# Attention over 64 heads: eleven pairs transposed by transfers inside SBUF, thirteen groups of scores on VectorE

## The chip, the cores and the metric

The kernel runs on one core of a Trainium2 chip. The metric is the device time of one execution in microseconds (us); a kernel's time is the median of several runs. A profiled execution gives the trace that is quoted here. The engines are called PE (matmuls; PEld is its weight load), ACT (exponentials), DVE (elementwise work), POOL (casts) and SP (issues transfers).

## What is computed

Plain attention for batch 8, 8 heads, 512 positions, dimension 64, in float32. So there are 64 independent heads.

```python
scores = np.einsum('bhqd,bhkd->bhqk', q, k) * scale
scores = scores - scores.max(axis=-1, keepdims=True)
attn = np.exp(scores)
attn = attn / attn.sum(axis=-1, keepdims=True)
return np.einsum('bhqk,bhkd->bhqd', attn, v)
```

The kernel leaves out the subtraction of the maximum, which changes nothing in exact arithmetic, and divides by the sum at the end: the values carry a column of ones, so that the sum comes out of the same matmul.

## The kernel before

**Pairs, groups, units.** The 64 heads are worked on as 32 pairs g. For each pair, q, k and v come from memory as one transfer per tensor (256 KB, `load`, L536 to L542, issued by SP), are cast to fp16 by POOL (`cast`, L544; v into `vp` at L548, q and k side by side into one tile `qkp` at L565), and q and k are transposed, so that the dimension lies along the partitions (`tqk`).

**Two ways to transpose.** Pairs 1 to 28 go through PE: `transposes` (L582 to L592) issues two sets of four 128x128 transposes into a PSUM bank, and `copy` (L601) brings the result to `tqk` with one DVE copy. Pairs 29 to 31 (`FLIPPED = 29`) go through `flip` (L594 to L599): one transposing transfer on SP's queue from `qkp` to `tqk`, both in SBUF. Pair 0 has a written-out start (`first_pair`).

**Scores.** A group m is two 128x512 blocks of scores (keys by queries), one of each head of the pair, four groups to a pair (m // 4 is the pair). PE writes it into one of three PSUM buffers `st` (`scores`, L618, matmuls at L642). ACT then takes the exponential of the whole group, `pt<-st`, at L647. That is the rule; the groups listed in `Plan.ON_DVE` have their exponential made on DVE instead, from a polynomial and the bits of the number: PE first adds a constant (the lift, L628), then `raise_` (L665) and three passes (`pass_`, L687) follow on DVE, with the result in `pd`. Each of them reads or writes 128x1024 elements. For a group in `Plan.SHARED` the middle pass runs on POOL (`middle`, L700 and L703). For a group in `SHARED` or `FREED` the score buffer comes free after the first pass, otherwise after the second. For a pair with such a group POOL also scales part of k (L564).

**Values.** For each head, four units of four matmuls multiply 128x128 pieces of the exponentials by v (`values`, L740), seven units to a PSUM bank; two banks `x0`, `x1` are shared by these and by the transposes. DVE takes the reciprocal of the sums (L708) and multiplies (L716) into a ring of 56 units in SBUF, from which SP stores finished heads (L731). ACT may run far ahead of the values: there are 30 `pt` tiles.

**The order of the work.** Nothing is scheduled at run time. The class `Plan` steps through a model of the engines in time, with its own constants for what each operation costs, and writes down a list of steps; the loop at the end of the kernel issues them in that order, and each engine works through its own queue in that order, waiting where data is not there. So the constants at the head of `Plan` decide which instruction stands ahead of which on each engine. The ones that the change touches:

- `due` (in `__init__`) sorts the casts: k and q of a pair are due `lead` before its scores (2300 ns, or `LEAD` = 8000 for a flipped pair), v later.
- `emit` writes down a cast; behind the cast of a flipped pair's q it writes the flip, and behind each cast the load that takes over the raw buffer (7 pairs later, `RAW`). From the time `CALM` on, a cast is made to wait for the DVE instruction before it (`cast_behind`, L577).
- `fits` holds a cast of q or k back until pair g - 5 is transposed (five `qkp` tiles).
- `step_sp` models SP's queue in order: a flip waits for both casts, and what stands behind it waits too.
- `step_pe` chooses between scores, transposes and values; `KEEN` is the group before which no values are begun; `HURRY`, `SOON`, `BACKLOG` say how long PE holds back for scores.
- `step_dve` chooses among copies, reciprocals, normalisations, raises and passes; `LATE_COPY`, `LATE_NORM`, `LATE_MULT` say how long these may be put off for a pass, and `ROOM` when a reciprocal is issued ahead of its multiplication.

```python
# the tiles between the steps (inside the kernel function)
lpool = ctx.enter_context(tc.tile_pool(name="load", bufs=7))
qpool = ctx.enter_context(tc.tile_pool(name="qk16", bufs=5))
tpool = ctx.enter_context(tc.tile_pool(name="tqk", bufs=6))
ppool = ctx.enter_context(tc.tile_pool(name="pt", bufs=30))
```

Of the kernel before, what the change touches and what calls it, by code (L numbers as in the profile page):

```python
# [17 lines left out]
class Stores:  # L18

    def __init__(self, pairs, units):  # L20
        self.pairs, self.units = pairs, units
        self.started = []
        self.waiting = []
# [24 lines left out]
class Plan:  # L48
# [7 lines left out]
    COPY_1 = (400, 190)  # L56
    NORM_COLUMN, PASS_DONE = 67, 80
    RECIP, RECIP_DONE, CHAINED = 80, 230, 117
    APART, ROOM = 1, -400
    PASS, PASSES = 1131, 3  # L60
    OFFSET = 216
    FIRST_EXP = 5130
    STEP = 5
    CALM, KEEN = 14000, 6
    FIRST_UNIT, FIRST_VALUES = 4, 6000
    ON_DVE = (9, 18, 28, 39, 49, 57, 68, 79, 89, 94, 103, 111)
    SHARED = (39, 49, 89, 103)
    FREED = (94, 111)

    LATE_NORM, LATE_MULT, LATE_COPY, HURRY, SOON, BACKLOG = 1300, 1600, 2200, 800, 40, 1500  # L70
    SLACK, AHEAD = 200, 2

    CAST, CAST_DONE, TO_POOL = 560, 130, 150
    SCALED, MORE = 595, 75
    MIDDLE, MIDDLE_DONE = (1120, 2300), 250
    FIRST_LAND, LOAD, STORE, LATENCY, ISSUE, FLIP_ISSUE = 5200, 700, 350, 2300, 540, 1490
    RAW, QK16, NV = 7, 5, 12
    FLIPPED, LEAD, FLIP = 29, 8000, 3500
    RING = 56

    def __init__(self, groups, pairs, first):
        self.groups, self.pairs = groups, pairs
        self.pe, self.act, self.dve = 6500, self.FIRST_EXP, 6500
        self.pool, self.port, self.dma = 4900, 4900, self.FIRST_LAND
        self.m, self.tiled = first, True
        self.buffers = [1e9] * 3
        self.buffer = {}
        self.exps = {}
        for m in range(first):
            self.act += self.EXP + self.EXP_FIXED  # L90
            self.exps[m] = self.buffers[m] = self.act + self.EXP_DONE
        self.tq = {0: 5800}
        self.transposed = {0: 5800}
        self.next_t = 1
        self.part_t = 0
        self.banks = [5100, 5800]
        self.todo = [(g, h) for g in range(pairs) for h in range(2)]
        self.last = self.todo.pop()
        self.last_part = 0
        self.head = None  # L100
        self.stores = Stores(pairs, self.RING)
        self.units = self.FIRST_UNIT
        self.member = {b: m for m, grp in enumerate(groups) for b in grp}
        self.ready = []
        self.passes = []
        self.steps = []
        self.busy_dve = 0
        self.done_heads = 0

        late = {grp[0][0] for m, grp in enumerate(groups) if m in self.ON_DVE}  # L110
        due = []
        for g in range(pairs):
            scores = 5000 + 3380 * g
            if g:
                lead = self.LEAD if g >= self.FLIPPED else 2300
                due += [(scores - lead, g, "k"), (scores - lead + 10, g, "q")]
            values = 4000 if g else self.FIRST_VALUES
            due.append((scores + values + (6000 if g in late else 0), g, "v"))
        self.due = sorted(due)
        self.extra = {}  # L120
        for m in self.ON_DVE:
            g = groups[m][0][0]
            self.extra[g] = self.extra.get(g, self.SCALED - self.MORE) + self.MORE
        self.uncast = list(self.due)
        self.casts = []
        self.landed, self.cast_done = {}, {}
        self.first_loads = [(g, n) for _, g, n in self.due if g < self.RAW]
        self.first_loads += [(self.RAW, "k"), (self.RAW, "q")]
        for x in self.first_loads:
            self.dma += self.LOAD  # L130
            self.landed[x] = self.dma
        self.loads = []
        self.sp = 1650 + 470 * len(self.first_loads)
# [4 lines left out]
    def released(self, m):  # L138
        return 0 if m in self.SHARED or m in self.FREED else 1

# [3 lines left out]
    def emit(self, t, after):  # L144
        _, g, n = self.uncast.pop(0)
        shared = (g, n) == (1, "q")
        self.note(t, "cast", g, n, t > self.CALM)
        if not shared:
            self.casts.append((g, n, t if after is None else after + self.TO_POOL))
        if n == "q" and g >= self.FLIPPED:  # L150
            self.note(t, "flip", g)
            self.loads.append(("flip", g))
        if g + self.RAW < self.pairs:
            self.note(t, "load", g + self.RAW, n)
            self.loads.append(("load", g + self.RAW, n))
# [25 lines left out]
    def step_sp(self, t):  # L181
        if not self.loads or self.sp > t:
            return
        what = self.loads[0]
        if what[0] == "flip":
            g = what[1]
            if any(self.cast_done.get((g, n), 1e9) > t for n in "kq"):
                return
            self.dma = max(self.dma, t + 1600) + 1000
            self.tq[g] = self.transposed[g] = max(self.dma, t + self.FLIP)  # L190
            self.loads.pop(0)
            self.sp = t + self.FLIP_ISSUE
            return
        elif what[0] == "load":
            _, g, n = what
            if g >= self.RAW and self.cast_done.get((g - self.RAW, n), 1e9) > t:
                return
            self.dma = max(self.dma, t + self.LATENCY - self.LOAD) + self.LOAD
            self.landed[(g, n)] = self.dma
        else:  # L200
            if what[1] > t:
                return
            self.dma = max(self.dma, t + self.LATENCY - self.STORE) + self.STORE
        self.loads.pop(0)
        self.sp = t + self.ISSUE
# [11 lines left out]
    def for_dve(self, m):  # L217
        return m in self.ON_DVE

# [29 lines left out]
    def transposes(self, t):  # L249
        if self.part_t == 0:  # L250
            self.bank_t = self.bank(t)
            self.banks[self.bank_t] = 1e9
        self.note(t, "transposes", self.next_t, self.part_t, self.bank_t)
        self.full(t, self.TRANSPOSE)
        self.part_t += 1
        if self.part_t == 2:
            self.transposed[self.next_t] = self.pe + self.TO_DVE
            self.ready.append((self.pe + self.TO_DVE, "copy", (self.next_t, self.bank_t)))
            self.next_t += 1
            self.part_t = 0  # L260

    def wants(self, g, h, part):
# [66 lines left out]
    def step_pe(self, t):  # L329
        if self.m == len(self.groups):  # L330
            self.values(t)
            return
        g = self.groups[self.m][0][0]
        backlog = self.act - t
        one, two = self.free() <= t, self.free(1) <= t
        if one and (two or backlog < self.HURRY or self.tiled):
            return self.scores(t)
        if not one and backlog < self.BACKLOG and self.free() < t + self.SOON:
            return
        if self.part_t:  # L340
            return self.transposes(t)
        if (
            self.next_t < min(self.pairs, self.FLIPPED)
            and self.next_t <= g + self.AHEAD
            and all(self.cast_done.get((self.next_t, n), 1e9) <= t for n in "kq")
            and self.bank(t) is not None
        ):
            return self.transposes(t)
        if not self.values(t) and one:
            self.scores(t)  # L350

    def step_dve(self, t):
# [56 lines left out]
        elif any(x[2] <= t for x in self.passes):  # L409
# [5 lines left out]
            if all(x[0] > end - late[x[1]] for x in self.ready):  # L415
# [11 lines left out]
                del self.passes[after]  # L427
                if s == 0 and m in self.SHARED:
                    self.passes.remove((m, 1, 1e9))
# [24 lines left out]
def kernel(  # L454
# [28 lines left out]
    raises = {}  # L483
    for m in Plan.ON_DVE:
        (g, c, _), (g2, c2, _) = groups[m]
# [3 lines left out]
    cpool = ctx.enter_context(tc.tile_pool(name="const", bufs=1))  # L489
    lpool = ctx.enter_context(tc.tile_pool(name="load", bufs=7))  # L490
    qpool = ctx.enter_context(tc.tile_pool(name="qk16", bufs=5))
    tpool = ctx.enter_context(tc.tile_pool(name="tqk", bufs=6))
    ppool = ctx.enter_context(tc.tile_pool(name="pt", bufs=30))
    dpool = ctx.enter_context(tc.tile_pool(name="pd", bufs=4))
    wpool = ctx.enter_context(tc.tile_pool(name="work", bufs=2))
# [15 lines left out]
    tqk = {}  # L511
# [61 lines left out]
    def dve(ins):  # L573
        latest[:] = [ins]
        return ins
# [99 lines left out]
    def pass_(m, s):  # L675
# [7 lines left out]
        last = s == 2  # L683
        shared = m in Plan.SHARED
        one = low if m not in Plan.FREED else f
        dve(
# [196 lines left out]
    with tc.manual_schedule():  # L883
# [10 lines left out]
        for n in range(NV):  # L894
            nc.vector.memset(vps[n][:, :, :, D : D + 1], 1.0)
        first_pair()
        do = {
            "transposes": transposes,
            "flip": flip,
            "scores": scores,  # L900
# [45 lines left out]
```

## Time and profile before

| | us |
|---|---|
| median of three runs | 117.22 (116.72 to 117.48) |
| the profiled execution | 117.66 |
| its span, first to last instruction | 115.9 |
| ACT busy | 108.4 |
| PE busy | 105.5 |
| DVE busy | 100.2 |
| POOL busy | 75.8 |

The profiled execution is 0.44 us above the median, and 1.8 us of it lie outside the span. In the lines that follow, a group of instructions shows its line in the kernel, engine and operation, what it writes and reads, its count, then busy time and the mean duration of one in ns, then the idle time of its engine ahead of it and what ended that. A line of a timeline begins with the start and the duration in us; consecutive instructions of a kind are merged. A line of windows shows for each engine the busy time in that stretch and the number of instructions, in the order PE, PEld, DVE, ACT, POOL, then the granted clock of PE, the share of the DMA engines that was busy (it can be over 1 where packets overlap) and GB/s. The granted clock was 1.00 throughout.

### The profile page before, as it was taken

The numbers are of one execution on the slowest core, as the hardware profiler recorded it, in microseconds if no ns is written. First come the engines' busy times: TensorE is split into PE (matmuls) and PEld (weight loads), VectorE is DVE, ScalarE is ACT, GpSimd is POOL, SyncE is SP. The second block draws the span as 40 slices with busy tenths as digits, with TensorE's granted clock in tenths as the row PEclk, the third lists the DMA queues.
The fourth block names the chain that finished last, engine by engine and source line by source line (L and its number), as shares of the span: only waits on it lengthen the run. The fifth ranks groups of instructions, "written<-read, shape, count | busy, mean of one in ns | idle before, by whom it ended". The sixth has DMA issues, their size and how long they took to land.

```text
span 115.9 us, 4036 instructions
## 1 busy us (share of the span) xinstructions
PE 105.5 (91%) x1558; PEld 65.8 (57%) x1558; DVE 100.2 (86%) x181; ACT 108.4 (94%) x120; POOL 75.8 (65%) x122
## 2 busy tenths in 40 slices
PE   7978989989998999999899998989999989799980
PEld 2454655556573668665575664756566556467660
DVE  4752599999999978999999999999999997997481
ACT  2589999999999999999999999999999999999980
POOL 2339965895985985999676949948792849821000
PEclk9999999999999999999999999999999999999999
DMA  3899999999999999999999999999927598026443
GB/s 91 293 305 373 384 379 382 384 377 381 363 384 374 375 378 374 369 371 359 351 380 375 385 377 311 375 367 377 382 100 206 182 119 224 2 96 228 145 159 112
DMA packets 38581, 34.61 MB, mean 299 GB/s; under 512 B 5409, under 2 KB 38561, under 8 KB 38561
## 3 DMA queue, kind: packets, MB, share of 16 engines
q1 hardware_dynamic: 37984, 34.02, 88.3%
q10 hardware_dynamic: 576, 0.33, 0.9%
q8 instruction: 12, 0.20, 0.7%
q14 instruction: 9, 0.07, 0.2%
HBM read 25.17 MB, written 8.39 MB: 290 GB/s over the span
## 4 chain that ended last, share of the span: by engine, by line
ACT 48%; PE 35%; issue 6%; DMA 5%; POOL 2%; SPq 2%; DVE 1%; ACTq 0%
ACT pt L647 48%; PE o L740 15%; PE st L642 14%; PE tp L590 5%; DMA k<-in_k_dram 5%; SPq L785 1%; POOL qkp L565 1%; PE st L628 1%; SPq L542 1%; DVE obl L771 1%; POOL vp L548 0%; POOL k L564 0%; DVE rc_last L770 0%; PE o_last L756 0%; ACTq L647 0%
## 5 line engine op out<-in xcount | busy, mean ns | idle before, releaser
L647 ACT ACTIVATE pt<-st 128x1024 f16<-128x1024 f32 (+1 forms) x114 | 103.9, 1153 | 0.3 <-PE st L642 0.3
L642 PE MATMUL st<-tqk 64*128 64x512 f16 (+1 forms) x250 | 46.1, 380 | 4.4 <-ACT pt L647 3.2
L740 PEld LDWEIGHTS <-pt 128*128 128x128 f16 x912 | 36.0, 98 | 15.9 <-issue 14.7
L740 PE MATMUL o<-vp,pt 128*128 128x65 f16 x912 | 43.9, 194 | 0.3 <-POOL vp L548 0.2
L548 POOL CAST vp<-v 128x512 f16<-128x512 f32 x32 | 19.4, 619 | 8.1 <-DVE pd L687 4.7
L716 DVE TENSOR_TENSOR ring<-o,rc 128x448 f32<-128x448 f32 (+2 forms) x37 | 22.6, 611 | 1.2
L642 PEld LDWEIGHTS <-tqk 64*128 64x128 f16 x250 | 13.4, 93 | 15.4 <-issue 7.0
L565 POOL CAST qkp<-k 128x512 f16<-128x512 f32 x31 | 19.0, 614 | 4.4 <-PE st L642 1.6
L565 POOL CAST qkp<-q 128x512 f16<-128x512 f32 x30 | 18.5, 616 | 5.0 <-DVE y L687 1.7
L610 DVE COPY tqk<-tp 128x1024 f16<-128x1024 f16 x27 | 18.3, 679 | 3.1 <-PE tp L590 3.1
L590 PE MATMUL tp<-ident,qkp 128*128 128x128 f16 x224 | 17.9, 220 | 0.6 <-DVE tqk L610 0.4
L590 PEld LDWEIGHTS <-qkp 128*128 128x128 f16 x224 | 12.8, 97 | 7.7 <-issue 3.6
L665 DVE TENSOR_SCALAR z<-st 128x1024 f32<-128x1024 f32 x12 | 14.6, 1218 | 2.0 <-PE st L642 2.0
L687 DVE SCALAR_TENSOR_TENSOR pd<-y,z 128x1024 uint32<-128x1024 f32 x12 | 15.1, 1258 | 0.0
L740 PE MATMUL o<-vp,pd 128*128 128x65 f16 x96 | 14.8, 195 | 0.0
L687 DVE SCALAR_TENSOR_TENSOR y<-st,z 128x1024 f32<-128x1024 uint16 x12 | 14.5, 1212 | 0.1
L740 PEld LDWEIGHTS <-pd 128*128 128x128 f16 x96 | 9.4, 98 | 1.3 <-issue 1.3
L708 DVE RECIPROCAL rc<-o 128x7 f32<-128x7 f32 (+2 forms) x37 | 7.2, 196 | 2.9 <-PE o L740 2.9
L703 POOL TENSOR_TENSOR y<-t,y 128x1024 f32<-128x1024 f32 x4 | 9.5, 2363 | 0.3
L564 POOL TENSOR_SCALAR k<-k 128x128 f32<-128x128 f32 x12 | 6.4, 530 | 4.2 <-DVE pd L687 2.5
L687 DVE SCALAR_TENSOR_TENSOR y<-st,y 128x1024 f32<-128x1024 uint16 x6 | 7.3, 1214 | 0.0
L628 PE MATMUL st<-const-bfloat16-1.0,lift 64*128 64x512 bf16 x24 | 4.6, 380 | 1.0 <-ACT pt L647 1.0
(57 smaller groups left out, 35.5 us busy)
## 6 DMA issues: line engine op xcount, KB each, us to landing
v<-in_v_dram SPq DMA_DIRECT2D x32, 256.0 KB, 5.4
k<-in_k_dram SPq DMA_DIRECT2D x31, 256.0 KB, 5.4
q<-in_q_dram SPq DMA_DIRECT2D x31, 256.0 KB, 5.4
out_dram<-ring SPq DMA_DIRECT2D x25, 256.0 KB, 4.9
out_dram<-ring SPq DMA_DIRECT2D x13, 128.0 KB, 4.6
k<-in_k_dram ACTq DMA_DIRECT2D x2, 64.0 KB, 2.4
q<-in_q_dram SPq DMA_DIRECT2D x2, 64.0 KB, 2.2
q<-in_q_dram SPq DMA_DIRECT2D x1, 128.0 KB, 3.2
```

The source lines that it names most:

```text
L548: return nc.gpsimd.tensor_copy(out=vps[g % NV][:, :, :, 0:D], in_=raw[g]["v"][:, :, :, :])
L565: ins = nc.gpsimd.tensor_copy(out=dst, in_=src[:, :, :, :])
L590: nc.tensor.transpose(tps[g][:, n, i, :], qkp[g][:, n, i, :], ident)
L610: nc.vector.tensor_copy(out=tqk[g][:, :, :], in_=tps.pop(g).rearrange("p n i c -> p n (i c)"))
L642: nc.tensor.matmul(st[:, x, cols], kc, qc[:, cols], start=not on_dve, stop=True)
L647: nc.scalar.activation(out=pt[:, :, cols], in_=st[:, :, cols], func=EXP, scale=scale)
L665: nc.vector.tensor_scalar(out=r["z"][:, :, :], in0=r["st"][:, :, :], scalar1=128.0, scalar2=2.0**17, op0=AluOp.mult, op1=AluOp.max,)
L687: nc.vector.scalar_tensor_tensor(out=r["bits"][:, :, :] if last else y, in0=(low, one, y)[s], scalar=(QUARTIC if shared else CUBIC)[s], in ...
L703: nc.gpsimd.tensor_tensor(out=y[:, :, :], in0=t[:, :, :], in1=y[:, :, :], op=AluOp.mult)
L708: dve(nc.vector.reciprocal(out=rcs[u][:, 0:n], in_=o[:, x : x + n, D : D + 1]))
L716: nc.vector.tensor_tensor(out=ring[:, u % NU : u % NU + n, :], in0=o[:, x : x + n, 0:D], in1=rc[:, 0:n].broadcast_to([P, n, D]), op=AluOp. ...
L740: nc.tensor.matmul(os[u // 7][:, u % 7, :], blocks[(g, c, h)][:, y * P : (y + 1) * P], vps[g % NV][:, h, c, :], start=(c == 0), stop=(c == ...
```

## The change

Eleven pairs, and not the last three alone, are transposed by transfers: 14, 17, 20, 22, 24 and 26 to 31. There are thirteen groups on DVE for twelve, at other places; two of them, and not four, share their middle pass with POOL, and four, not two, are in `FREED`. The planner's account of a transposing transfer is 1400 ns of the queue's time and 500 ns behind it, for 1000. Other constants of the planner change as listed, and `tqk` has ten buffers for six. The instructions themselves stay as they are.

```diff
-    APART, ROOM = 1, -400
+    APART, ROOM = 1, 600
...
-    CALM, KEEN = 14000, 6
+    CALM, KEEN = 9000, 7
     FIRST_UNIT, FIRST_VALUES = 4, 6000
-    ON_DVE = (9, 18, 28, 39, 49, 57, 68, 79, 89, 94, 103, 111)
-    SHARED = (39, 49, 89, 103)
-    FREED = (94, 111)
-
-    LATE_NORM, LATE_MULT, LATE_COPY, HURRY, SOON, BACKLOG = 1300, 1600, 2200, 800, 40, 1500
-    SLACK, AHEAD = 200, 2
+    ON_DVE = (8, 18, 28, 38, 45, 55, 65, 70, 80, 91, 97, 105, 112)
+    SHARED = (65, 97)
+    FREED = (55, 91, 105, 112)
+
+    LATE_NORM, LATE_MULT, LATE_COPY, HURRY, SOON, BACKLOG = 1600, 1600, 1400, 800, 0, 800
+    SLACK, AHEAD = 300, 2
...
-    FLIPPED, LEAD, FLIP = 29, 8000, 3500
+    FLIPPED = (14, 17, 20, 22, 24, 26, 27, 28, 29, 30, 31)
+    LEAD, FLIP = 8000, 3500
...
-                lead = self.LEAD if g >= self.FLIPPED else 2300
+                lead = self.LEAD if g in self.FLIPPED else 2300
...
-        if n == "q" and g >= self.FLIPPED:
+        if n == "q" and g in self.FLIPPED:
             self.note(t, "flip", g)
             self.loads.append(("flip", g))
...
-            self.dma = max(self.dma, t + 1600) + 1000
-            self.tq[g] = self.transposed[g] = max(self.dma, t + self.FLIP)
+            self.dma = max(self.dma, t + 1600) + 1400
+            self.tq[g] = self.transposed[g] = max(self.dma + 500, t + self.FLIP)
...
             self.next_t += 1
+            while self.next_t in self.FLIPPED:
+                self.next_t += 1
...
-            self.next_t < min(self.pairs, self.FLIPPED)
+            self.next_t < self.pairs
...
-    tpool = ctx.enter_context(tc.tile_pool(name="tqk", bufs=6))
+    tpool = ctx.enter_context(tc.tile_pool(name="tqk", bufs=10))
```

## The prediction

> **What bounds the kernel now.** I read the page first (busy time, then the chain that ended last), then the timeline of ScalarE, then busy times by stage, then the groups of what the change touches, and last the transfers around the three transposing ones that exist already.
>
> The page:
>
> ```profile
> PE 105.5 (91%) x1558; PEld 65.8 (57%) x1558; DVE 100.2 (86%) x181; ACT 108.4 (94%) x120; POOL 75.8 (65%) x122
> ...
> DMA  3899999999999999999999999999927598026443
> ...
> ACT 48%; PE 35%; issue 6%; DMA 5%; POOL 2%; SPq 2%; DVE 1%; ACTq 0%
> ```
>
> See that ACT and PE share the chain, that DVE is at 86% only because it idles at both ends, and that the DMA engines are full until slice 29 (85 us).
>
> ScalarE's timeline, whole and in a stretch without gaps:
>
> ```profile
> 8.35 5.62 ACT L647 ACTIVATE pt<-st 128x1024 f16<-128x1024 f32 x6
> 14.26 98.25 ACT L647 ACTIVATE pt<-st 128x1024 f16<-128x1024 f32 x108 [0.28 <-PE st L642]
> ...
> 19.70 5.66 ACT L647 ACTIVATE pt<-st 128x1024 f16<-128x1024 f32 x6
> ```
>
> Exponentials overlap: one of them lasts about 1.15 us, and six take 5.66 us, so a new one starts every (5.66 - 1.15) / 5 = 0.90 us. At that step 106 whole ones from 14.26 us on take 95.8 us, the two half ones about 1.2 us, together 97.0 of 98.25 us: ACT never stands idle long, and late starts cost it 1.2 us in all. ACT bounds the kernel. What can be won is the exponentials taken from it and those 1.2 us.
>
> Busy times by stage:
>
> ```profile
> 15.00:50.00 35.00, 33.09 (x506) 21.11 (x506) 33.34 (x51) 35.00 (x40) 26.92 (x44) 1.00 1.08 376
> 50.00:85.00 35.00, 33.53 (x506) 21.00 (x503) 34.33 (x52) 35.00 (x40) 27.70 (x42) 1.00 1.06 364
> 85.00:105.00 20.00, 18.30 (x292) 11.66 (x293) 19.16 (x30) 20.00 (x23) 12.42 (x17) 1.00 0.53 124
> 105.00:116.00 11.00, 7.60 (x151) 5.34 (x147) 5.59 (x15) 7.51 (x10) 0.00 (x0) 1.00 0.50 165
> ```
>
> Columns: PE, PEld, DVE, ACT, POOL busy, granted clock, DMA share, GB/s. DVE (third) has 1.7 us of idle time from 15 to 50 us and 1.5 us from 50 to 105. PE has 1.9 and 3.2.
>
> **The change part by part.** The groups it touches:
>
> ```profile
> L610 DVE COPY tqk<-tp 128x1024 f16<-128x1024 f16 x27 | 18.3, 679 | 3.1 <-PE tp L590 3.1
> L590 PE MATMUL tp<-ident,qkp 128*128 128x128 f16 x224 | 17.9, 220 | 0.6 <-DVE tqk L610 0.4
> L687 DVE SCALAR_TENSOR_TENSOR pd<-y,z 128x1024 uint32<-128x1024 f32 x12 | 15.1, 1258 | 0.0
> L703 POOL TENSOR_TENSOR y<-t,y 128x1024 f32<-128x1024 f32 x4 | 9.5, 2363 | 0.3
> ```
>
> *One more group of scores on VectorE (13 for 12).* ACT loses one exponential: -0.90 us on the path. DVE gains a group. PE gains two lift matmuls (the chain has two as 0.22 us), beside the rest.
>
> *DVE's sum.* Its instructions overlap a little: by its timeline a pass starts the next 1.13 us later and a copy 0.60 us later. A group takes four instructions (raise and three passes), a shared one three, the middle pass being POOL's. Before: 8 x 4 + 4 x 3 = 44. After, with two shared: 11 x 4 + 2 x 3 = 50. So 6 x 1.13 = +6.8 us, and eight copies fewer, 8 x 0.60 = -4.8 us: +2.0 us against 3.2 us of idle time from 15 to 105 us. It is uneven. Groups 38 and 45 stand where shared 39 and 49 stood, so the first half gains two passes, +2.3 us, against 1.7 us of idle time and the 0.9 us that starting at group 8 and not 9 opens. The second half gains 4 x 1.13 = 4.5 and loses 4.8. DVE is then full from 13 us to 105 us; I cost this at nothing because what waits for it (normalised outputs, last passes) has PE's backlog of values between it and ACT. If that cover is gone, each us of DVE too many is a us of the end (below).
>
> *Transposes off PE.* Eight pairs more (14, 17, 20, 22, 24, 26, 27, 28) lose eight transposes each; the chain shows such a set as 0.55 us, so PE loses 4.4 us and gains 0.22, all of it after 45 us. This is off ACT's path except where ACT starts late for want of scores. Of the 1.2 us of late starts, some 0.9 lie after 45 us, in about eight places of 0.1 each, most at a group that DVE holds. Bounds: nothing, if all come from the buffer that DVE holds, and -0.9, if all come from PE's load. I take -0.4, between the ends, since the chain does run through PE at those places (57.5 to 69.9, 82.3 to 89.1, 104.3 to 109.4 us). A thirteenth place of the kind: +0.1.
>
> *POOL.* Two middles fewer, 2 x (1.05 + 2.36) = -6.8 us, one scaling of k more, +0.53: off the path at 65%.
>
> *Planner constants, casts and queues.* Values begin one group later, casts wait for DVE from 9 us on, the limits for late copies and norms move. A flipped pair's casts are due 8.0 us before its scores, not 2.3, so they go ahead of those of an unflipped pair before it, and the loads issued behind those casts move with them. On POOL nothing is added. The one stretch where such order shows in ACT is 13 to 14.3 us, 0.4 us late: -0.4 to +0.4, taken at zero, as no row tells the sign. Ten tqk buffers for six cost nothing and take away a wait of transfers for scores long done.
>
> *The eight transfers.* What the three that exist did, by SP's timeline:
>
> ```profile
> 86.28 1.33 SPq L596 DMA_TRANSPOSE tqk<-qkp  x1
> 87.71 4.24 SPq L731 DMA_DIRECT2D out_dram<-ring  x5
> 92.24 4.24 SPq L596 DMA_TRANSPOSE tqk<-qkp  x2
> ```
>
> By the transfers' line, their landing after issue:
>
> ```profile
> DMA to landing us min/median/max: 2.8/2.9/4.5
> ```
>
> By windows of 1 us (last columns: DMA share, GB/s):
>
> ```profile
> 93.00:94.00 1.00, 0.89 (x17) 0.57 (x14) 1.00 (x2) 1.00 (x3) 0.35 (x1) 1.00 1.85 202
> 94.00:95.00 1.00, 0.63 (x6) 0.36 (x6) 1.00 (x3) 1.00 (x3) 0.40 (x1) 1.00 0.98 38
> ```
>
> Each holds SP 1.3 us, once 2.6 (a load 0.4 to 0.7), so SP gains 8 x 1.3 = 10 us, while a full DMA queue of some 5 us (loads land 5.4 us after issue) covers each. The first one, alone, moved its packets in 1.1 us; the second, behind stores, had the DMA engines nearly stuck for a us (38 GB/s) and took about 3. So eight cost 8.8 to 24 us of DMA time. The DMA engines have room: after 85 us they move 3.5 MB of stores, 9.3 us at 376 GB/s, and three transfers, 5.2 us, which leaves 28 - 14.5 = 13.5 us before 113 us. And loads lie early: by issue and landing, pair 14's keys land at 34 us for scores at 51, pair 24's at 62 for 84, pair 31's at 82 for 108. I take 1.1 to 1.7 us each (the mean of the three is 5.2 / 3), 8.8 to 13.6 us, hidden.
>
> The Trainium skill's page "Advanced Engine Details and Errata", section "X-Bar Transpose (TRN2)", says that a transposing transfer is as fast as a plain one. The trace disagrees: 1.1 us against 0.70 us for the same 262 KB at 376 GB/s; by the page eight would take 5.6 us, and nothing else here would change.
>
> Sum: -0.90 - 0.4 + 0.1 = -1.2 us. The profiled execution took 117.66 us, 115.9 of span and 1.8 around it, 0.44 over the median 117.22. 117.66 - 1.2 = 116.46, and 116.0 beside the median.
>
> **The rivals.**
>
> *A: transfers crowd the DMA queue (slower).* Place: SP and DMA, 45 to 110 us. A transfer waits on SP for its pair's casts with the loads behind it waiting too (the first of the three stood there 5.3 us, by SP's waits), and between stores it stalls the engines. It decides from 13.5 / 8 = 1.7 us each. At 2.2 us the room is overrun by 8 x 2.2 - 13.5 = 4 us, so 117.2 - 0.9 + 4 = 120.3. For it: the mean of the three lies right at the limit. Against: one of the three stalled, and loads have 17 to 25 us of lead, which absorbs 3 us each for six transfers before 85 us. Beside it, the Trainium skill ("VectorE: DVE Perf Modes", section "The three transpose paths") advises TensorE for a 128x128 transpose where PSUM will do; its 1309 ns per block by DMA would make eight blocks 10.5 us, and 2.9 us from issue to landing says no.
>
> *B: DVE becomes the bound.* For: +2.0 us on an engine with 3.2 us left, over by 0 to 0.6 us in the first half. Groups 38 and 45 hold their score buffer through a second pass, 1.13 us longer. If none of the idle time can be used and the thirteenth group costs its 0.1, the end moves by 2.0 + 0.1 - 0.9: 118.4. Against: the 1.3 us idle before 13.4 us and 2.5 us after 105.
>
> *C: only the exponential is won.* Late starts stay, a thirteenth is added: 117.2 - 0.9 + 0.1 = 116.4, within 1%.
>
> *D: all late starts after 45 us go, and the early one:* 117.2 - 0.9 - 0.9 - 0.4 = 115.0.
>
> **How the numbers follow.** Forecast and its neighbourhood (115.4 to 116.5) 0.42, C 0.18, D 0.06, A 0.22, B 0.12. About 1% (1.2 us) is what a measurement of this kernel can tell from no change, so 116.0 stands on the line. Faster, below 116.05: 0.36 of the forecast's 0.42, and D: 0.42. Within 1%: the forecast's other 0.06, C, 0.01 of A and half of B: 0.31. Slower, above 118.4: 0.21 of A and half of B: 0.27. Range: from 115.2, under the forecast's own and above D, up into A to 119.6, which leaves out D and 0.14 of A. The likeliest case alone spans 115.4 to 116.5.
>
> **What would show it.** ACT: one exponential fewer, still at a 0.90 us step, late starts of 0.7 to 1.3 us: right. DVE: no gap between 15 and 105 us and still no wait of ACT. DMA: full to 93 us or so. Wrong, and A: gaps of several us in ACT or PE behind transfers or casts after 50 us, DMA full to the end, stores late. Wrong, and B: PE waiting on DVE's outputs and a longer stretch after the last exponential (3.4 us now).

## The result, and the profile after

The changed kernel took 121.33 us (median of four, 119.65 to 122.96) where the kernel before took 116.97; their ratio is 1.0255, 95% interval 1.0202 to 1.0308. Run again beside later experiments it took 120.96 us (120.24 to 121.21), ratio 1.0328 (1.0290 to 1.0366). The forecast was 116.0, its range 115.2 to 119.6. The ratios leave out disturbed executions, here two of the four (122.07 us and the first profiled one, 122.96 us), so that 1.0255 is less than 121.33 / 116.97, and the changed kernel's lines below are those of the second profile, an execution of 120.24 us with a span of 118.5 us.

Its page, the lines that answer to the first fence of the prediction, with the granted clock:

```profile
PE 103.5 (87%) x1496; PEld 63.4 (54%) x1496; DVE 102.4 (86%) x179; ACT 107.9 (91%) x119; POOL 71.4 (60%) x119
...
PEclk9999999999999999999999997699999999999997
DMA  3999999999999999999999989999999999797353
...
ACT 43%; PE 22%; DVE 13%; issue 8%; DMA 8%; POOL 3%; SPq 1%; POOLq 0%; ACTq 0%
```

ACT has lost an exponential, and DVE has 2.2 us more work where 2.0 were forecast. PE has only 2.0 us less, where the forecast had 4.4 less and 0.22 more. The DMA engines are full to slice 34 (101 us) and not to slice 29. DVE has entered the chain (13%, 1% before), and DMA has 8% of it for 5%, half of that stores. The clock dips in slices 25 and 26.

ScalarE's timeline:

```profile
8.36 60.60 ACT L650 ACTIVATE pt<-st 128x1024 f16<-128x1024 f32 x66
71.04 3.07 ACT L650 ACTIVATE pt<-st 128x1024 f16<-128x1024 f32 x3 [2.08 <-PE st L645]
74.82 1.02 ACT L650 ACTIVATE pt<-st 128x1024 f16<-128x1024 f32 x1 [0.70 <-PE st L645]
76.26 38.76 ACT L650 ACTIVATE pt<-st 128x1024 f16<-128x1024 f32 x43 [0.42 <-PE st L645]
```

All is as forecast to 69 us, and from 76 us on again. Between them lies one hole: 2.08 us without an exponential, then two smaller gaps. Summed over all its starts, ACT comes 5.0 us late (1.5 in the kernel before, counted alike from its first start). The tail after the last exponential is 3.4 us, as before.

Busy times by stage:

```profile
15.00:50.00 35.00, 31.68 (x447) 19.17 (x445) 34.29 (x48) 35.00 (x39) 25.32 (x46) 1.00 1.10 362
50.00:85.00 35.00, 31.52 (x473) 19.53 (x469) 31.21 (x48) 31.75 (x35) 23.79 (x36) 0.95 1.14 331
85.00:105.00 20.00, 18.36 (x290) 11.37 (x288) 19.76 (x30) 20.00 (x23) 13.68 (x18) 1.00 1.19 272
```

In the second line ACT loses 3.2 of 35 us, and DVE and PE idle with it; the DMA share is over 1.1 while the bytes fall to 331 GB/s. Where the hole comes from is read backwards, first from PE:

```profile
67.30 0.39 PE L645 MATMUL st<-tqk 64*128 64x512 f16 x2
68.67 0.40 PE L593 MATMUL tp<-ident,qkp 128*128 128x128 f16 x4 [0.98 <-POOL qkp L568]
70.22 0.40 PE L593 MATMUL tp<-ident,qkp 128*128 128x128 f16 x4 [1.15 <-POOL qkp L568]
70.55 0.39 PE L645 MATMUL st<-tqk 64*128 64x512 f16 x2
```

PE works in order. Transposes of pair 21, one that still goes through PE, wait for its casts, and the scores behind them wait too, 67.7 to 70.55 us. POOL:

```profile
53.06 0.61 POOL L568 CAST qkp<-q 128x512 f16<-128x512 f32 x1
59.36 0.61 POOL L568 CAST qkp<-k 128x512 f16<-128x512 f32 x1 [5.68 <-DMA tqk<-qkp]
...
65.70 2.35 POOL L706 TENSOR_TENSOR y<-t,y 128x1024 f32<-128x1024 f32 x1
68.01 0.61 POOL L568 CAST qkp<-k 128x512 f16<-128x512 f32 x1
68.56 1.60 POOL L568 CAST qkp<-q 128x512 f16<-128x512 f32 x1
```

POOL stood still for 5.68 us until a transfer landed and gave its `qkp` buffer free, then had its casts and the middle pass of group 65 to catch up, and came to pair 21's casts at 68 us. The transfer on SP, and then the landing of all eleven:

```profile
52.47 1.86 SPq L599 DMA_TRANSPOSE tqk<-qkp  x1
```

```profile
DMA to landing us min/median/max: 3.8/5.9/7.1
```

It was issued at 52.47 us and landed at 59.2, 6.8 us later, with seven other transfers issued and not yet landed. Last, windows of 2 us over the hole (third value from the right: the granted clock):

```profile
68.00:70.00 2.00, 0.40 (x4) 0.23 (x4) 1.60 (x1) 0.96 (x2) 2.00 (x3) 1.00 0.74 179
70.00:72.00 2.00, 1.55 (x18) 0.85 (x19) 1.35 (x3) 0.96 (x1) 1.78 (x4) 1.00 1.09 385
72.00:74.00 2.00, 2.00 (x24) 0.97 (x22) 2.00 (x3) 1.95 (x3) 0.75 (x2) 0.63 1.09 383
74.00:76.00 2.00, 2.00 (x24) 1.13 (x21) 0.99 (x3) 1.14 (x2) 1.04 (x2) 0.52 1.58 245
```

PE did 0.40 us of work in the first two, and from 72.5 us on its clock was halved for 3.4 us; the two smaller gaps of ACT lie there. The matmuls are longer at half clock, which is part of why PE's sum fell by so little: with the transfers left out (below) it is 101.5 us.

### The profile page after: what moved, and what is told of

The parts are those of the page before. It is cut to its first block, busy times and chain, and to the rows that moved or that the text cites. A ratio compares the mean times of both kernels' runs of the same rounds, so it can differ in the third digit from the quotient of the medians.

```text
span 121.0 us, 3918 instructions
## 1 busy us (share of the span) xinstructions
PE 104.7 (87%) x1496; PEld 63.7 (53%) x1496; DVE 103.3 (85%) x179; ACT 108.5 (90%) x119; POOL 73.3 (61%) x119
## 4 chain that ended last, share of the span: by engine, by line
ACT 30%; DVE 20%; PE 19%; issue 9%; DMA 8%; POOL 8%; SPq 2%; POOLq 0%; ACTq 0%
ACT pt L650 30%; PE o L743 9%; PE st L645 8%; DVE ring L719 5%; DMA out_dram<-ring 4%; DMA k<-in_k_dram 4%; DVE z L668 4%; DVE y L690 3%; POOL qkp L568 3%; POOL y L706 3%; DVE pd L690 3%; DVE tqk L613 2%; DVE rc L711 2%; PE tp L593 1%; SPq L788 1%
## 5 line engine op out<-in xcount | busy, mean ns | idle before, releaser
L743 PE MATMUL o<-vp,pt 128*128 128x65 f16 x904 | 46.4, 198 | 0.4 <-DVE tqk L613 0.2
L743 PEld LDWEIGHTS <-pt 128*128 128x128 f16 x904 | 37.4, 100 | 16.5 <-issue 15.7
L568 POOL CAST qkp<-q 128x512 f16<-128x512 f32 x30 | 21.4, 712 | 2.5 <-DVE pd L690 1.4
L690 DVE SCALAR_TENSOR_TENSOR pd<-y,z 128x1024 uint32<-128x1024 f32 x13 | 17.1, 1315 | 0.5 <-POOL y L706 0.3
L743 PE MATMUL o<-vp,pd 128*128 128x65 f16 x104 | 16.8, 200 | 0.2 <-DVE pd L690 0.2
L690 DVE SCALAR_TENSOR_TENSOR y<-st,z 128x1024 f32<-128x1024 uint16 x13 | 15.7, 1209 | 0.1
L613 DVE COPY tqk<-tp 128x1024 f16<-128x1024 f16 x19 | 12.8, 673 | 3.2 <-PE tp L593 3.2
L593 PE MATMUL tp<-ident,qkp 128*128 128x128 f16 x160 | 12.8, 220 | 2.6 <-POOL qkp L568 2.4
L593 PEld LDWEIGHTS <-qkp 128*128 128x128 f16 x160 | 9.2, 97 | 7.2 <-POOL qkp L568 3.7
L690 DVE SCALAR_TENSOR_TENSOR y<-z,y 128x1024 f32<-128x1024 uint16 x4 | 5.3, 1318 | 0.0
```

What stands on the lines that cost most here:

```text
L568: ins = nc.gpsimd.tensor_copy(out=dst, in_=src[:, :, :, :])
L593: nc.tensor.transpose(tps[g][:, n, i, :], qkp[g][:, n, i, :], ident)
L613: nc.vector.tensor_copy(out=tqk[g][:, :, :], in_=tps.pop(g).rearrange("p n i c -> p n (i c)"))
L690: nc.vector.scalar_tensor_tensor(out=r["bits"][:, :, :] if last else y, in0=(low, one, y)[s], scalar=(QUARTIC if shared else CUBIC)[s], in ...
L743: nc.tensor.matmul(os[u // 7][:, u % 7, :], blocks[(g, c, h)][:, y * P : (y + 1) * P], vps[g % NV][:, h, c, :], start=(c == 0), stop=(c == ...
```

## The experiments

Two theories stood first. **Q**: the transfers do the harm, by what they do to the DMA queue and by those who wait for them. **V**: VectorE's sum or the planner's new constants do it, and the transfers are harmless. Ratios are to the kernel before, run beside each, with 95% intervals.

**The transfers alone** (the changed kernel with the old groups and constants):

```diff
-    ON_DVE = (8, 18, 28, 38, 45, 55, 65, 70, 80, 91, 97, 105, 112)
+    ON_DVE = (9, 18, 28, 39, 49, 57, 68, 79, 89, 94, 103, 111)
...
```

> The eleven transfers alone, with the groups and constants of the kernel before. Theory Q (transfers stand behind some seven queued loads and stores, land 6 to 7 us after issue, and hold casts, scores and stores up meanwhile): clearly slower than before, 119 to 121 us, landing 6 us or more in the middle, POOL idle for us at a time on a transfer. Theory V (VectorE is over its time, or the new constants order the work badly; the transfers are harmless): 116.5 to 117.5 us, no long wait on a transfer.

124.02 us, ratio 1.0503 (1.0413 to 1.0593). V fails as the whole answer, and the loss is larger than the 119 to 121 us that Q gave. In the profile, an execution of 124.60 us, the transfers landed 2.7 to 6.9 us after issue, and ACT was 6.7 us late in all.

**The groups and constants alone:**

```diff
-    FLIPPED = (14, 17, 20, 22, 24, 26, 27, 28, 29, 30, 31)
+    FLIPPED = (29, 30, 31)
```

> The thirteen groups and the new constants alone, with the three transfers of before (pairs 29 to 31). Theory Q: 116.0 to 117.0 us, an exponential saved. Theory V: slower still than the changed kernel or as slow, 119 us or more, because VectorE gets eight copies (4.8 us) back on top of the thirteenth group.

121.42 us, ratio 1.0381 (1.0329 to 1.0434). Q's figure fails here, V's holds: each half of the change is slower without the other. The last exponential ended at 111.7 us, 0.9 us earlier than before, but 7.4 us of values and outputs were left behind it (3.4 before). The chain of this kernel:

```profile
PE 46%; ACT 44%; issue 4%; DMA 2%; DVE 1%; ACTq 0%
```

The values left at the end are PE's work. DVE, with 6.8 us more and no copies taken off, was busy 19.73 of 20 us from 85 to 105 us; that its load put the values off is argued, not shown.

**Eight buffers for the cast q and k:**

```diff
-    qpool = ctx.enter_context(tc.tile_pool(name="qk16", bufs=5))
-    tpool = ctx.enter_context(tc.tile_pool(name="tqk", bufs=10))
+    qpool = ctx.enter_context(tc.tile_pool(name="qk16", bufs=8))
+    tpool = ctx.enter_context(tc.tile_pool(name="tqk", bufs=9))
```

> The changed kernel with eight buffers for the cast q and k in place of five (and nine, not ten, for the transposed ones, for room); the order of the work is the same. Tests one branch of theory Q, that a late transfer keeps its input buffer and so stops POOL's casts (5.7 and 2.9 us in the trace). If that branch is the larger part: 117.0 to 118.0 us and no ScalarE gap at 70 us. If late scores and late stores are the larger part: 119 to 120 us. Theory V: no change from the changed kernel.

122.1 us, ratio 1.0407 (1.0345 to 1.0469). This is above both of the expected figures. POOL's wait for a transfer is gone, and no time is won: other waits took its place. By the waits between 80 and 92 us, PE stood for late transfers:

```profile
PEld L645 <- DMA tqk<-qkp: 1.8, 1, 1.8
PE st L645 <- DMA tqk<-qkp: 1.7, 1, 1.7
```

and over the whole run DVE waited 2.3 us for late stores to give its output ring free. The chain, too, goes through transfers more than in the changed kernel (DMA 18%, 14% of it stores, where the changed kernel has 8%):

```profile
ACT 31%; DVE 24%; PE 18%; DMA 18%; issue 6%; POOL 1%; SPq 0%; DVEq 0%; ACTq 0%
```

So the held buffer is the first of several places that lose time, not the whole cause.

**Less in the DMA queue** (the loads of v from pair 7 on are left out), in the changed kernel and, as its control, in the kernel before:

```diff
         for name in names:
+            if name == "v" and g >= 7:
+                raw.setdefault(g, {})["v"] = raw[g % 7]["v"]
+                continue
```

> The changed kernel without the loads of v from pair 7 on (the old values are used again, so this part of the work is left out); all else stays in its order. The DMA queue then carries 6.5 MB less. Theory Q: transfers land within 3 to 5 us, no ScalarE gaps after 50 us, 115.5 to 116.5 us. Theory V: 119 us or more, as VectorE and the order are untouched.

> The kernel before without the loads of v from pair 7 on (that part is left out), the control for the same cut in the changed kernel. ScalarE bounds it, and its transfers of the end do not meet loads: 116.6 to 117.3 us, as before. If the cut itself won time (less waiting of any kind), it would be under 116.2 us, and the 117.0 us of the changed kernel with that cut would be worth less than it looks.

116.99 us, ratio 0.9999 (0.9971 to 1.0028); the control 117.9 us, ratio 1.0057 (1.0036 to 1.0078). Leaving out these loads wins nothing by itself, it even costs a little, and it brings the changed kernel back to the time of before, half a microsecond above the range that Q gave. Order and groups were untouched, so the loss goes with the load of the queue. The transfers landed after 4.3 us (median), where the changed kernel has 5.9.

**The transfers left out** (scores of those pairs are made from an earlier pair's transposed tile):

```diff
     def flip(g):
+        tqk[g] = tqk[max(tqk)]
+        return
```

> The changed kernel with all eleven transfers left out: their pairs' scores are made from the transposed q and k of an earlier pair, so this part of the work is left out and everything else stands in the same order. If the transfers alone carry the loss: no ScalarE gap over 0.4 us after 15 us, DMA engines with idle time from about 85 us, 115.8 to 116.8 us. If VectorE's sum (+2.0 us) or the constants carry part of it: 117.5 us or more, with a tail after the last exponential longer than 3.5 us.

116.53 us, ratio 0.9946 (0.9917 to 0.9975). So without any of its eleven transfers the change is worth 0.6 us. ACT's late starts were 1.2 us in all, its tail 3.6 us, DVE was 34.24 of 35 us busy in each of the two middle stages.

> The changed kernel unaltered, on the chip of its neighbours here, to have them side by side: 119.6 to 122 us.

This is the repetition told of above: 120.96 us. So the eleven transfers cost 4.4 us (120.96 - 116.53).

**Capacity or lateness?** The planner was given what a transfer had taken, and in a second kernel the casts were put earlier:

```diff
-    LEAD, FLIP = 8000, 3500
+    LEAD, FLIP = 8000, 7000
...
-            self.dma = max(self.dma, t + 1600) + 1400
+            self.dma = max(self.dma, t + 1600) + 2000
```

> The changed kernel with the planner told what a transfer took: 7.0 us from issue to landing in place of 3.5, and 2.0 us of the queue in place of 1.4; all else follows from its plan. Theory L (latency: the work is ordered for transfers that land in 3.5 us, and stands waiting for those that take 6 to 7): most of the loss comes back, 116.5 to 118 us. Theory C (capacity: eight more transfers of 2.0 us each are 16 us of DMA time where 13.5 us were free, whatever the order): 119 to 121 us, with the DMA engines full to about 108 us.

```diff
-    LEAD, FLIP = 8000, 3500
+    LEAD, FLIP = 12000, 3500
```

> The changed kernel with the casts of the transferred pairs due 12 us ahead of their scores in place of 8. Theory L: transfers land before their scores, 117 to 118.5 us. Theory C: no better than the changed kernel, 119 to 122 us, since each microsecond of lead takes buffers from the pairs between and no DMA time is won.

Ratios 1.0252 (1.0209 to 1.0295) and 1.0376 (1.0309 to 1.0443). Neither helped; POOL's wait of 5.7 us was still in the first, as the planner holds a cast back for the pair five before it, and casts no longer go in the order of pairs.

Fewer transfers, late ones only, with the old groups (five) and with the new (seven):

```diff
-    FLIPPED = (14, 17, 20, 22, 24, 26, 27, 28, 29, 30, 31)
+    FLIPPED = (27, 28, 29, 30, 31)
```

> Groups and constants of the kernel before, with five transfers in place of three, those of pairs 27 to 31, when the loads are nearly through. Theory C: 2 more times 2 us are well inside the 13.5 us, so 116.5 to 117.4 us, as before. Theory L: these too stand behind loads for 5 us or more where the plan says 3.5; 117.5 us or more.

```diff
-    FLIPPED = (14, 17, 20, 22, 24, 26, 27, 28, 29, 30, 31)
+    FLIPPED = (25, 26, 27, 28, 29, 30, 31)
```

> The changed kernel with seven transfers, all at the end (pairs 25 to 31). Theory C: 4 x 2.0 = 8 us of 13.5, no overrun; VectorE gains 6.8 us and loses only four copies (2.4 us) against 3.2 us of idle time, so 1.2 us too much: 117 to 118.2 us with full VectorE at the end. Theory L: transfers of 25 to 28 stand behind the last loads, 118.5 us or more with ScalarE gaps after 85 us.

Five: 1.0242 (1.0152 to 1.0331), against theory C, for two more transfers, well within the room, cost some 2 per cent, though the interval is wide. Seven: 120.26 us, 1.0262 (1.0245 to 1.0279), with ACT no later than before (1.6 us) but the outputs too late, as in the kernel with groups alone. Here DVE is on the chain, and from 95 us on it has nearly half of it. Of this kernel, the chain, ACT and then DVE:

```profile
PE 38%; ACT 37%; DVE 15%; issue 6%; ACTq 0%
```

```profile
8.39 103.39 ACT L650 ACTIVATE pt<-st 128x1024 f16<-128x1024 f32 x113
```

```profile
114.01 0.42 DVE L719 TENSOR_TENSOR ring<-o,rc 128x256 f32<-128x256 f32 x1
```

ACT is done at 111.8 us and the last output is only made at 114.4. (Theory C had 118.2 at most, so VectorE's overrun was set too low.) Each theory had thus missed: lateness in the two kernels first told of, and in the gaps of ACT that it foresaw for the last; room in the one with five.

**Plain copies in place of the transfers**, same bytes, order, waits and buffers:

```diff
-        nc.sync.dma_start_transpose(
-            out=tqk[g][:, :, :].rearrange("p n (i c) -> p (n i) c", c=P),
-            in_=qkp[g][:, :, :, :].rearrange("p n i c -> p (n i c)"),
-        )
+        nc.sync.dma_start(
+            out=tqk[g][:, :, :], in_=qkp[g][:, :, :, :].rearrange("p n i c -> p n (i c)")
+        )
```

> The changed kernel with a plain copy of the same 256 KB from the cast tile to the transposed one in place of each of the eleven transfers (so the transposing is left out; order, waits and buffers are the same). Tells the DMA time of a transposing transfer (2.0 us in the full queue) from the waiting in the queue, which a plain copy has too. If the time it takes is the cause: 7.7 us of DMA time in all in place of 22, 116.2 to 117.2 us. If standing behind seven transfers while holding buffers is the cause: landing 5 to 6 us after issue as for loads, and 118.5 us or more.

117.37 us, ratio 1.0011 (0.9982 to 1.0040), just above the range set for time in the queue and well under that for waiting. The copies too stand in the queue:

```profile
DMA to landing us min/median/max: 2.4/5.3/5.7
```

and POOL still waited 4.1 us at the same place, but ACT's hole was 0.7 us where it was 2.08. The same stretch of time in windows, the changed kernel and then this one:

```profile
44.00:92.00 48.00, 43.96 (x676) 27.78 (x676) 44.14 (x66) 44.75 (x50) 33.06 (x52) 0.96 1.14 320
```

```profile
44.00:92.00 48.00, 45.45 (x721) 28.92 (x720) 46.17 (x72) 47.21 (x52) 35.15 (x55) 1.00 1.07 372
```

At 320 GB/s the changed kernel moved 15.36 MB in 48 us, of which six transfers are 1.57. The other 13.8 MB take 36.7 us at 376 GB/s, which leaves 11.3 us, by this estimate 1.9 us for each transfer. With plain copies the queue runs at 372 GB/s. The two pages, again the changed kernel first, show the same bytes in far more packets:

```profile
DMA packets 47011, 36.69 MB, mean 310 GB/s; under 512 B 13840, under 2 KB 46992, under 8 KB 46992
```

```profile
DMA packets 36979, 36.69 MB, mean 318 GB/s; under 512 B 2400, under 2 KB 35552, under 8 KB 36960
```

That is 11,440 more packets under 512 B, 1,040 for each transposing transfer. A plain copy also holds SP for less time, and that is a rival. But in windows of 4 us from 44 to 92 us the DMA share of the changed kernel was never under 0.91 and mostly over 1, so SP's longer hold did not run the queue dry.

**Five late transfers with eight buffers:**

```diff
-    qpool = ctx.enter_context(tc.tile_pool(name="qk16", bufs=5))
-    tpool = ctx.enter_context(tc.tile_pool(name="tqk", bufs=10))
+    qpool = ctx.enter_context(tc.tile_pool(name="qk16", bufs=8))
+    tpool = ctx.enter_context(tc.tile_pool(name="tqk", bufs=9))
```

> Groups and constants of before, five late transfers, with eight buffers for the cast q and k (nine for the transposed). With five buffers POOL waited 2.6 us for a transfer just ahead of the shared group's middle pass. If that held buffer is the cause of its 2 to 3 per cent: 116.5 to 117.4 us. If the transfers' lateness for the scores or the stores is: 118.5 us or more.

117.53 us, ratio 1.0036 (1.0015 to 1.0057), 0.1 us above the expected range, where five buffers gave 1.0242. With few transfers the held buffer is nearly all of the loss: POOL's wait for it had put a middle pass, and then the casts, late.

**More shared groups in place of transfers**, thirteen groups, six of them shared, the three transfers of before:

```diff
-    SHARED = (65, 97)
-    FREED = (55, 91, 105, 112)
+    SHARED = (28, 45, 55, 70, 91, 105)
+    FREED = (112,)
```

> Thirteen groups with only the three transfers of before, six of them with the middle pass on POOL in place of two: VectorE then has 7 x 4 + 6 x 3 = 46 instructions for groups where the kernel before has 44, +2.3 us in place of +6.8, and POOL gains 4 x 3.4 us against 40 us of idle time. If VectorE's sum is what the transfers had to pay for, this needs no transfer: 116.0 to 117.5 us, tail after the last exponential under 4 us. If the groups' places or the constants are at fault: 119 us or more, as with two shared groups (121.4 us).

123.63 us, ratio 1.0577 (1.0531 to 1.0624): ACT stood 5.3 us at 67 us, for scores. So the thirteenth group did not come free by way of POOL either. POOL was 71% busy over the run, and at casts after casts just ahead of the gap. Which of its delays made the hole is not shown.

## Why the prediction was wrong, point by point

- **The exponential, -0.90 us: right.** ACT has 113 starts of its line for 114, still at 0.90 us steps.
- **PE's transposes, -0.4 us of late starts: not borne out.** With no transfer in the way ACT's late starts were 1.2 us against 1.5, the early and the later ones together. The kernel before without its later loads of v has 1.1 us, counted alike, with all its transposes still on PE, so the 0.3 us can't be put down to PE's lighter load. The rest of the change comes out like rival C: 116.4 forecast for it, 116.53 measured.
- **VectorE's +2.0 us, hidden: right, and only because of the copies.** The tail after the last exponential did not grow (3.4 to 3.6 us). Where copies stayed (three or seven transfers) it grew to 7.4 and 6.9 us, and the kernels were 3.8 and 2.6 per cent slower: the longer tail of rival B, at another number of copies. With seven DVE is on the chain; with three PE's values are, and DVE's part is argued.
- **The eight transfers, hidden at 1.1 to 1.7 us each: the step that failed.** They were put at nothing in the sum, and all eleven cost 4.4 us. The term was mis-sized: about 1.9 us each in a full queue. The lowest of the three samples had been taken in an empty queue, and the row with 38 GB/s for a whole microsecond was the nearer one, for the eight added ones run among loads. The room was wrongly counted too: 13.5 us free after 85 us are of no use to transfers that stand among loads at 44 to 90 us. The queue was full to 101 us, where the prediction had 93.
- **What is late next was not priced.** The prediction looked at the lead of the loads, and that held: pair 31's keys landed at 88.5 us in the first profile for scores at 113. It named the ten `tqk` buffers and passed over the five of `qkp`. A transfer holds one from the cast until landing, and that is longer than its time in the queue: pair 17's q was cast by 45.7 us, SP, in order and behind with its loads, issued the transfer at 52.5, and it landed at 59.2. POOL, also in order, stands behind it with the casts of the other pairs. From the copies: a plain transfer's time and its waiting in the queue cost 0.8 us (117.37 - 116.53), and the transposing, with the longer waits that it makes, 3.6 us more (120.96 - 117.37). The three were not run side by side, but their ratios (0.9946, 1.0011, 1.0328) say the same.
- **Rival A** had the place and the sign, and 120.3 us at 2.2 us each was near the mark. A gap of ACT behind casts after 50 us was among its signs and is there (2.08 us). But the mechanism that priced it, room overrun to the end, is not what the trace shows: the tail did not grow, and the time was lost in the middle. That its figure comes near is luck.
- **A transposing transfer against a plain one.** The Trainium skill, "Advanced Engine Details and Errata", section "X-Bar Transpose (TRN2)", has a transposing transfer as fast as a plain one. Against plain copies at the same place the runs show about 1.9 us for 0.70 (262 KB at 372 GB/s), and the measurement decides.

That the transfers caused the loss is shown twice, by leaving them out and by the lighter queue; that it is the transposing more than the place in the queue, by the copies. With eleven transfers, how the loss divides among held buffers, late scores and late stores is not shown: with one branch mended, the others took over. No kernel that computes the whole result beats the one before; 0.6 us is what this way would win if its transfers cost nothing.

## What to carry to other kernels

Price a transfer by what it takes in the queue that it will stand in, not by a sample from an empty one, and ask of it what it holds while it waits: here the source buffer mattered before the data did. Room on a shared queue counts only where and when the transfer runs. A change whose parts pay for each other should be costed part by part: here VectorE needed the copies gone, and what took them off cost more than the exponential saved.

## What the runs showed of the hardware that was not expected

- A transposing transfer of 256 KB moved in about 1,040 packets under 512 B, and held SP 1.24 to 3.5 us, against 0.5 us for a plain copy of the same tiles (0.47 to 0.64 us).
- PE's clock may be halved after a short starvation, and need not be. In the profile shown PE had 0.98 and 1.15 us without work, four transposes between them, and from 72.5 us ran for 3.4 us at a granted clock of 0.5, in which a pair of scores matmuls 0.39 us long took 0.52 to 0.64. In the first profile the same place had 0.83 and 1.16 us without work, and the clock stayed at 1.00; so it did after 2.15 us without work in the kernel with casts 12 us ahead. The Trainium skill, "TensorE: Matmul & The Clock Gate", section "What's actually happening", gives an idle window of about 3.4 us as the trigger, and as much of sustained work to come back. The second agrees; for the first, the trace shows 2.9 us between scores with eight transposes inside, and no idle stretch over 1.2 us. What decides between the cases is not shown.
